# Pairs of up tiles by seven products in the first quarter of the MLP, sums of x behind the activations, and value products by twos

## The chip, the cores and the metric

The kernel runs on one core of a Trainium2 chip. The metric is the device time of one execution in microseconds. The engines are TensorE (PE in the profile; PEld is its loading of weights), VectorE (DVE), ScalarE (ACT), GpSimd (POOL) and SyncE (SP), which only issues transfers. Each engine takes its instructions in the order in which the program has them, and waits for another by semaphores.

## The reference

One inference step of a two-layer encoder with D = 1024 features and 576 tokens (512 of a prompt, 64 of a running stream). Layer 0 mixes tokens by causal pooling over windows, layer 1 by sparse attention: an indexer selects keys, then softmax attention with 16 heads, 4 key heads, runs over them. Each layer is followed by an MLP with squared ReLU. Cut to what matters here:

```python
h = _rmsnorm(x, g)                       # x: 576 x 1024
u = jnp.square(jax.nn.relu(h @ w_up))    # 1024 -> 4096
x = x + u @ w_down                       # 4096 -> 1024
...
s = jnp.where(valid[:, :, None, None, :], s, NEG)
p = jax.nn.softmax(s, axis=-1).astype(v.dtype)
o = jnp.einsum('btgrk,btkgd->btgrd', p, vg)
```

## The kernel before

Features lie on the partitions and tokens in the free dimension: x is eight tiles of 128 x 576, handled in two halves of 288 tokens. Every product of the MLP is made in fp32r from operands that are split into an upper and a lower part, so that a product of a 128 x 128 block of weights with 288 tokens takes three matmuls (upper by upper, upper by lower, lower by upper). ScalarE casts the upper part (L192 for weights, L490 for activations), VectorE or GpSimd subtracts it to get the lower part (L193, L493). In the text a lower is that subtraction.

`mlp` goes over the 4096 hidden features in four quarters of eight up tiles, each followed by its share of the down product. In quarters 1 to 3 two up tiles make a pair, and `seven` gets a pair by seven products of half-size blocks where plain work has eight; the down products of all quarters are made so too. Such a group is 7 products x 4 tiles x 3 matmuls = 84 matmuls; two plain tiles are 96. The products, in the order of their work, are b11, t1, t2, b21, t3, b22, t4. Three PSUM banks (a, b, c) gather them. The operands t1, t2, t4 are sums of x: `x_sums` makes them for a tile j by one scaled copy on ScalarE (L449), four fused VectorE rows of 288 columns (L450 to L453), one cast of 864 columns (L454) and one lower of 864 columns (L455, tile xt). t3 is a difference, kept in `snap` (L451) and split by `x_difference` into the first half of xs[j], which the plain products read until then.

In the first quarter all eight up tiles are plain: `project` (L325) runs 8 x 3 x 2 = 48 matmuls a tile. The first two are done before the normalisation's factor is known: its statistics are asked for behind tile 1, and TensorE spreads the factor over the partitions (rb, L355) inside tile 2; ScalarE copies it to SBUF (rbm, L356). Then `finished` takes each tile: the activation (L477 for a tile in two banks, L479 for one in a pair of banks), which frees the tile's PSUM, the square (L471), the sums of the activations (L501 to L514) and their split. The sums of x follow behind tiles 3 and 5 (j = 0, 1), and inside the first two groups of down products (j = 2, 3, in `x_prepared`).

Weights come as a stream of blocks in the order of `mlp_jobs`. A block of kind "up" is used as it is. A pair of blocks, "even" and "odd", is turned into the seven weight operands of a pair: some of them are sums of blocks, made by accumulating transfers on GpSimd's queue (L234, L255) or by VectorE (L280, L284). `Stream.fill` issues the transfers as there is room.

A scheduler of the framework places the instructions on each engine; `behind` and `issue_after` put an instruction behind given others. The order in the built program therefore differs from that of the code.

In the attention, `values` (L1422, L1429, L1435) multiplies the probabilities with V, for each query block i and each key head group in two steps s = 0, 1. For i = 2, 3 each step writes half of a PSUM tile o with outputs of 64 partitions, two heads apart by 64; for the block of the running stream (i = 4) the last of five key tiles has 64 rows.

## Time and profile before

| what | before |
|---|---|
| time, median of 3 runs (lowest to highest) | 1066.94 us (1066.5 to 1067.46) |
| the profiled execution, in all | 1068.9 us |
| its span | 1065.8 us |
| mean granted TensorE clock | 0.995 |

The profile is of one execution, taken on the core. Its page gives the busy time of each engine, the chain of work that ended last, the costliest groups of instructions (line, engine, operation, output<-inputs, shape, count, then busy us, mean ns of one and idle us ahead of it with what ended it), and the transfers. Behind it the trace can be asked for the rows of any engine in a stretch of time, for the chain in order of time, and for a table of windows.

### The profile page before, as it was taken

Reading aid. Unit: us, or ns where it says so; the run is one execution under the profiler, and the core shown is the slowest. Engines: PE = TensorE matmul, PEld = TensorE weight load, DVE = VectorE, ACT = ScalarE, POOL = GpSimd, SP = SyncE. Lnnn points to the kernel's source line nnn. Section 1 sums busy time; section 2 is a strip of 40 time slices with the busy share of each in tenths; the row PEclk is TensorE's granted clock in tenths of the full one; section 3 lists DMA queues with packets and bytes.
Section 4 is the critical chain, followed back from the end, with each engine's and each line's share of the span. In section 5 each row is a group of like instructions: output and inputs, shape, how many; then the busy total and the mean of one; then the engine's idle time right before and its main releaser. Section 6 shows DMA issues by size and latency. Waiting matters only on the chain.

```text
span 1065.8 us, 21684 instructions
## 1 busy us (share of the span) xinstructions
PE 1045.2 (98%) x7970; PEld 1023.4 (96%) x7970; DVE 910.7 (85%) x1865; ACT 624.7 (59%) x1252; POOL 237.6 (22%) x254
## 2 busy tenths in 40 slices
PE   8999999999999999999999999999999999999996
PEld 8999999999999999999989889999999999999995
DVE  7879989879978998889999675689989979979984
ACT  8546557547646765354368786455467447547742
POOL 3200111111111110667556711000111111111101
PEclk9999999999999999999999999999999999999998
DMA  8334676676576665845542545343665676676522
GB/s 251 91 99 100 167 173 152 168 172 161 146 182 169 156 174 170 238 129 149 169 149 78 180 134 149 119 110 88 181 166 141 178 177 161 150 187 158 127 54 89
DMA packets 98027, 159.64 MB, mean 150 GB/s; under 512 B 15697, under 2 KB 29312, under 8 KB 97920
## 3 DMA queue, kind: packets, MB, share of 16 engines
q1 hardware_dynamic: 70720, 111.78, 33.3%
q0 software_dynamic: 15840, 28.84, 17.1%
q10 hardware_dynamic: 11360, 17.63, 5.2%
q8 instruction: 62, 1.02, 0.4%
q14 instruction: 45, 0.37, 0.1%
HBM read 142.99 MB, written 12.72 MB: 146 GB/s over the span
## 4 chain that ended last, share of the span: by engine, by line
PE 85%; DVE 7%; DMA 3%; issue 2%; POOL 2%; ACT 1%; SPq 0%; ACTq 0%; DVEq 0%; POOLq 0%
PE b L527 31%; PE c L527 16%; PE up L325 9%; PE a L527 8%; PE pj L325 5%; PE wo L325 3%; PE wa L325 2%; PE pb L1067 1%; PE pt L1397 1%; PE o L1429 1%; DMA raw<-in_w_in 1%; PE dn L325 1%; DVE mask L1314 1%; PE sc L1371 1%; DVE wl L193 1%
## 5 line engine op out<-in xcount | busy, mean ns | idle before, releaser
L192 ACT CAST wh<-raw 128x512 fp32r<-128x512 f32 x308 | 189.4, 619 | 196.0 <-PE b L527 63.2
L193 DVE TENSOR_TENSOR wl<-raw,wh 128x512 fp32r<-128x512 f32 x284 | 197.4, 697 | 33.7 <-ACT wh L192 29.4
L527 PE MATMUL b<-u,wh 128*128 128x288 f32 x992 | 202.1, 295 | 0.4 <-DVE u L493 0.4
L527 PEld LDWEIGHTS b<-u,wh 128*128 128x128 f32 x992 | 159.6, 188 | 1.3 <-DVE u L493 0.7
L192 ACT CAST wh<-sum 128x512 fp32r<-128x512 f32 x165 | 102.0, 620 | 95.2 <-PE b L527 33.7
L527 PE MATMUL b<-u,wl 128*128 128x288 f32 x496 | 145.3, 295 | 0.4 <-DVE wl L193 0.4
L193 DVE TENSOR_TENSOR wl<-sum,wh 128x512 fp32r<-128x512 f32 x165 | 112.1, 685 | 18.7 <-ACT wh L192 17.2
L527 PE MATMUL c<-u,wh 128*128 128x288 f32 x496 | 102.6, 296 | 0.0
L255 POOL DMA_DIRECT2D sum<-in_w_down x31 | 27.1, 894 | 327.4 <-DMA sum<-in_w_down 124.9
L527 PEld LDWEIGHTS b<-u,wl 128*128 128x128 f32 x496 | 93.2, 188 | 0.6 <-DVE wl L193 0.6
L325 PE MATMUL up<-xs,wh 128*128 128x288 f32 x512 | 89.3, 295 | 0.2
L493 DVE TENSOR_TENSOR u<-v,u 128x576 fp32r<-128x576 f32 (+3 forms) x106 | 82.7, 786 | 3.5 <-ACT u L490 3.1
L527 PEld LDWEIGHTS c<-u,wh 128*128 128x128 f32 x496 | 79.7, 188 | 1.3 <-ACT wh L192 1.1
L527 PE MATMUL b<-xt,wh 128*128 128x288 f32 x384 | 78.0, 296 | 1.3 <-DVE v L664 1.3
L527 PE MATMUL b<-xs,wh 128*128 128x288 f32 x384 | 77.3, 295 | 0.0
L490 ACT CAST u<-v 128x576 fp32r<-128x576 f32 (+3 forms) x106 | 73.4, 699 | 4.0 <-DVE v L514 3.2
L325 PEld LDWEIGHTS up<-xs,wh 128*128 128x128 f32 x512 | 74.7, 188 | 1.0 <-DVE v L479 0.7
L527 PE MATMUL c<-u,wl 128*128 128x288 f32 x248 | 73.2, 295 | 0.0
L255 POOL DMA_DIRECT2D sum<-in_w_up x24 | 20.8, 865 | 201.7 <-DVE wl L193 77.5
L527 PEld LDWEIGHTS b<-xt,wh 128*128 128x128 f32 x384 | 61.5, 188 | 1.8 <-DVE v L664 1.8
L325 PE MATMUL pj<-xs,wh 128*128 128x288 f32 x352 | 62.1, 295 | 0.0
L527 PEld LDWEIGHTS b<-xs,wh 128*128 128x128 f32 x384 | 61.2, 188 | 0.0
(298 smaller groups left out, 2723.4 us busy)
## 6 DMA issues: line engine op xcount, KB each, us to landing
raw<-in_w_up SPq DMA_DIRECT2D x128, 256.0 KB, 3.0
raw<-in_w_down SPq DMA_DIRECT2D x128, 256.0 KB, 2.8
raw<-in_w_o ACTq DMA_DIRECT2D x32, 256.0 KB, 2.7
sum<-in_w_down SPq DMA_DIRECT2D x31, 256.0 KB, 2.8
sum<-in_w_down POOLq DMA_DIRECT2D x31, 256.0 KB, 4.4
raw<-in_w_down POOLq DMA_DIRECT2D x31, 256.0 KB, 4.9
raw<-in_w_in ACTq DMA_DIRECT2D x30, 256.0 KB, 3.1
sum<-in_w_up SPq DMA_DIRECT2D x24, 256.0 KB, 3.0
```

What stands on the lines that cost most here:

```text
L192: cast(h, src)
L193: (sub or how["sub"]).tensor_tensor(l, src, f32(h), ALU.subtract)
L255: pool.dma_start(s1, odd[:, 512:], accum_op=ALU.add)
L325: pe.matmul(pt[h][:, :m] if isinstance(pt, tuple) else pt[:, h, :m], wt, xs[k][:, part, c:c + m], start=(k == 0 and i == 0), stop=(k == n ...
L490: return act.copy(u[:, f, 0], v[:, f])
L493: return dve.tensor_tensor(u[:, f, 1], v[:, f], f32(u[:, f, 0]), ALU.subtract)
L527: ins = pe.matmul(bank[:, :HT], wt, ut, start=first and j == 0 and i == 0, stop=j == 3 and i == 2, skip_group_check=True)
L1067: pe.matmul(pt[:, c0:c0 + rhs.shape[1]], lhs, rhs, start=n == 0, stop=n == len(steps) - 1)
L1314: dve.match_replace(order[rows], m8[rows], order[rows], TAKEN)
L1371: pe.matmul(pt[:, hh, :nw], q[:, 2 * s + hh], ks[g][:, part, :nw], start=part == 0, stop=part == 1)
L1397: pe.transpose(pp[:, c:c + P], pr[:, hh, kt * P:(kt + 1) * P], ident)
L1429: pe.matmul(o[64 * hh:64 * hh + 64, s * P:(s + 1) * P], V[:, kt, vs], pT[:, c:c + P], start=kt == 0, stop=kt == i)
```

## The change

Of the eight up tiles of each first quarter, the first four stay plain (`PLAIN_UP`); the last four become two pairs by `seven`, so that the stream's blocks of these are "even" and "odd". All sums and differences of x stand before those pairs: `x_sums(0)` behind the statistics' last sum, `x_sums(1)` and `x_sums(2)` behind the activation of tile 1, `x_sums(3)` at tile 3. The lowers of j = 0, 1 go to GpSimd; so does the second lower of three of the four plain blocks. The difference is written to `rough[:, j]`, and `x_prepared` is gone. Apart from the MLP, `values` makes both steps of a group at s = 1 for i = 2, 3, and the last key tile of i = 4 uses all 128 rows, those of the padding set to zero.

```diff
+PLAIN_UP = 4
+POOLED = (1, 2, 3)
...
-                kind = "odd" if c and n % 2 else "even" if c else "up"
+                kind = "up" if not c and n < PLAIN_UP else "odd" if n % 2 else "even"
...
+                if kind == "even" and "sums" not in phase:
+                    return
...
+                pooled = kind == "up" and (ups - 1) % PLAIN_UP in POOLED
...
-                dve.tensor_tensor(self.s2, self.s2, sq, ALU.add)
+                self.added = dve.tensor_tensor(self.s2, self.s2, sq, ALU.add).ins
...
-        def x_sums(j, raw, first, difference):
+        def x_sums(j):
...
+            at = half * (1 + j % 2)
+            raw, first, difference = rough[:, at:at + 3], rough[:, at + 3], rough[:, j]
...
-            dve.tensor_tensor(t[:, :, 1], raw, f32(t[:, :, 0]), ALU.subtract)
+            (pool if j < 2 else dve).tensor_tensor(t[:, :, 1], raw, f32(t[:, :, 0]), ALU.subtract)
...
-                dve.scalar_tensor_tensor(v, pt[:, :, :HT], 0.0, halves(norm.rb), ALU.max, ALU.mult)
+                active[:] = [dve.scalar_tensor_tensor(v, pt[:, :, :HT], 0.0, halves(norm.rb), ALU.max, ALU.mult).ins]
...
-        for i in range(KT):
+        for i in range(PLAIN_UP):
...
             if i == 1:
                 norm.stats()
+                with behind([norm.added]):
+                    x_sums(0)
             if i < 2:
                 continue
+            if i == 3:
+                x_sums(3)
             for t in todo:
                 finished(*t)
             todo.clear()
...
+            if i == 2:
+                snap = halves(tmp("snap", "s2", 1))
+                with behind(active):
+                    x_sums(1)
+                    x_sums(2)
+        for j in range(half):
+            x_difference(j, rough[:, j])
+        for j in range(PLAIN_UP // 2, half):
+            up = Up(0, j)
+            seven(of_x, False, up)
+            us.append(up.u)
...
-        for n, q in enumerate(FIRST_DOWN):
-            seven(of(us), n == 0, Down(q))
-            x_prepared(n)
+        for q in FIRST_DOWN:
+            seven(of(us), q == FIRST_DOWN[0], Down(q))
...
+        pool.memset(V[TS:, 8], 0.0)
...
+                        pool.memset(end[TS:, :4 * TS], 0.0)
...
-                if s == 0:
+                if s == (TURNED <= i < 4):
                     self.group.o = psum1("o")
+                if TURNED <= i < 4 and s == 0:
+                    self.group.pT = pT
+                    return
...
-                    for kt in range(i + 1):
-                        for hh in range(2):
-                            c = (kt * 2 + hh) * P
-                            pe.matmul(o[64 * hh:64 * hh + 64, s * P:(s + 1) * P], V[:, kt, vs], pT[:, c:c + P], start=kt == 0, stop=kt == i)
+                    for j, t in enumerate((self.group.pT, pT)):
+                        for kt in range(i + 1):
+                            for hh in range(2):
+                                c = (kt * 2 + hh) * P
+                                pe.matmul(o[64 * hh:64 * hh + 64, j * P:(j + 1) * P], V[:, kt, vs], t[:, c:c + P], start=kt == 0, stop=kt == i)
```

The lines of the kernel move by a few: the weight lower L193 becomes L195, the sums of x L450 to L455 become L460 to L465, the activations L477 and L479 become L489 and L491, the sums of activations L501 to L514 become L513 to L526, the matmuls L325 and L527 become L333 and L539, the split of xs L312 becomes L320, and the value products L1429 become L1437.

The first place is VectorE, from the first activation in the first quarter of layer 0 on. A number behind a name tells one buffer from another: up_687 and up_748 are tiles 0 and 1, up_832 and up_833 the two halves of tile 2. Before:

```order
L479 SCALAR_TENSOR_TENSOR v_891<-up_687,rbm_149_866 128x2x288
L479 SCALAR_TENSOR_TENSOR v_891<-up_748,rbm_149_866 128x576
L193 TENSOR_TENSOR wl_917<-raw_401,wh_916 128x512
L501 TENSOR_TENSOR v_891<-v_891 128x288
L508 SCALAR_TENSOR_TENSOR v_891<-v_891 128x288
L511 TENSOR_TENSOR v_891<-v_891 128x288
L514 SCALAR_TENSOR_TENSOR v_891<-v_891 128x288
L493 TENSOR_TENSOR u_892<-v_891,u_892 128x3x288
L493 TENSOR_TENSOR u_892<-v_891,u_892 128x4x288
L193 TENSOR_TENSOR wl_992<-raw_407,wh_991 128x512
L477 SCALAR_TENSOR_TENSOR v_905<-up_832,rbm_149_866 128x288
L477 SCALAR_TENSOR_TENSOR v_905<-up_833,rbm_149_866 128x288
```

With the change tiles 0 and 1 are up_677 and up_756, and tile 2 is up_845 and up_846. The order starts with the same activations:

```order
L491 SCALAR_TENSOR_TENSOR v_904<-up_677,rbm_151_879 128x2x288
L491 SCALAR_TENSOR_TENSOR v_904<-up_756,rbm_151_879 128x576
L460 SCALAR_TENSOR_TENSOR rough_676<-x_81,gv,rough_676 128x288
L461 SCALAR_TENSOR_TENSOR rough_676<-x_83,gv,rough_676 128x288
L460 SCALAR_TENSOR_TENSOR rough_676<-x_82,gv,rough_676 128x288
L461 SCALAR_TENSOR_TENSOR rough_676<-x_84,gv,rough_676 128x288
L195 TENSOR_TENSOR wl_945<-raw_731,wh_944 128x512
L513 TENSOR_TENSOR v_904<-v_904 128x288
L462 SCALAR_TENSOR_TENSOR rough_676<-x_83,negative_674,rough_676 128x288
L195 TENSOR_TENSOR wl_1048<-raw_733,wh_1047 128x512
L462 SCALAR_TENSOR_TENSOR rough_676<-x_84,negative_674,rough_676 128x288
L505 TENSOR_TENSOR u_905<-v_904,u_905 128x3x288
```

and comes to the activation of tile 2 (up_845, up_846) 18 rows further on:

```order
L195 TENSOR_TENSOR wl_1107<-raw_738,wh_1106 128x512
L465 TENSOR_TENSOR xt_932<-rough_676,xt_932 128x3x288
L460 SCALAR_TENSOR_TENSOR rough_676<-x_82,gv,rough_676 128x288
L505 TENSOR_TENSOR u_905<-v_904,u_905 128x4x288
L462 SCALAR_TENSOR_TENSOR rough_676<-x_84,negative_674,rough_676 128x288
L489 SCALAR_TENSOR_TENSOR v_918<-up_845,rbm_151_879 128x288
L489 SCALAR_TENSOR_TENSOR v_918<-up_846,rbm_151_879 128x288
L491 SCALAR_TENSOR_TENSOR v_918<-up_954,rbm_151_879 128x576
```

Before, eight rows stand between the activation of tile 1 and that of tile 2; now there are 27, among them the sums of x for j = 1, 2 and part of j = 3, the differences' lowers (L320) and five weight lowers.

The second place is TensorE behind tile 3 of the first quarter of layer 0. Before, the plain tiles follow one another (up_923 is tile 3, up_1006 tile 4):

```order
L325 MATMUL up_923<-xs_660,wh_742 128x288 x4
L325 MATMUL up_923<-xs_660,wl_743 128x288 x2
L325 MATMUL up_923<-xs_663,wh_742 128x288 x4
L325 MATMUL up_923<-xs_663,wl_743 128x288 x2
L325 MATMUL up_1006<-xs_642,wh_817 128x288 x4
L325 MATMUL up_1006<-xs_642,wl_818 128x288 x2
L325 MATMUL up_1006<-xs_645,wh_817 128x288 x4
L325 MATMUL up_1006<-xs_645,wl_818 128x288 x2
```

With the change the pair's products stand there (up_954 is tile 3; b_1031, a_1032, c_1033 are the banks of the first pair, xt_825, xt_924, xt_932 the sums of x for j = 0, 1, 2):

```order
L539 MATMUL a_1032<-xs_650,wh_944 128x288 x2
L539 MATMUL a_1032<-xs_650,wl_945 128x288
L539 MATMUL a_1032<-xs_653,wh_944 128x288 x2
L539 MATMUL a_1032<-xs_653,wl_945 128x288
L539 MATMUL b_1031<-xt_924,wh_940 128x288 x2
L539 MATMUL b_1031<-xt_924,wl_941 128x288
L539 MATMUL b_1031<-xt_932,wh_940 128x288 x2
L539 MATMUL b_1031<-xt_932,wl_941 128x288
L539 MATMUL c_1033<-xt_825,wh_841 128x288 x2
L539 MATMUL c_1033<-xt_825,wl_842 128x288
L539 MATMUL c_1033<-xt_924,wh_841 128x288 x2
L539 MATMUL c_1033<-xt_924,wl_842 128x288
```

The products t2 and t1 read xt_825, xt_924 and xt_932 within 21 matmuls of tile 3's end; before, the first products that read a sum of x stood behind the down products, a whole quarter later. The pair's first product (b_1031 from xs_632 to xs_641) stands ahead of tile 3.

The third place is TensorE in the attention, at a group of value products for i = 2. Before, the two steps of o_7715 stand apart:

```order
L1371 MATMUL sc_7700<-k_6064,q_7618 128x384 x4
L1429 MATMUL o_7715<-pT_7655,V 64x128 x6
L1397 MATMUL pt_7766<-ident,p_7627 128x128 x6
L1371 MATMUL sc_7776<-k_6064,q_7618 128x384 x4
L1429 MATMUL o_7715<-pT_7691,V 64x128 x6
L1397 MATMUL pt_7838<-ident,p_7663 128x128
```

With the change the two steps of a group, o_7820, follow each other:

```order
L333 MATMUL wa_7757<-ot_7687,wl_7065 128x256
L1437 MATMUL o_7820<-pT_7691,V 64x128 x6
L1437 MATMUL o_7820<-pT_7727,V 64x128 x6
L1374 MATMUL sc_7884<-k_6105,q_7724 128x384 x3
L1400 MATMUL pt_7901<-ident,p_7735 128x128 x4
L333 MATMUL wa_7833<-ot_7238,wh_7070 128x256 x2
```

The products of the first step moved behind the transposes of the second. Of the four groups of i = 2 one stood so before, and all four do now; in those of i = 3 other rows still stand between the steps.

More of the change, by code (lines that the diff above doesn't have):

```diff
@@ L262, in made @@
         stream = Stream()
+        ups = 0
         while True:
@@ L270, in made @@
                 turns["out"] += kind == "w_o"
+                if kind == "up":
+                    ups += 1
+                pooled = kind == "up" and (ups - 1) % PLAIN_UP in POOLED
                 for i in range(2):
-                    u = split_unit(raw[i], kind == "w_kq" and i == 0 and turns["spare"] < SPARE_UNITS, pool if early or kind == "w_kq" and i else None,
+                    u = split_unit(raw[i], kind == "w_kq" and i == 0 and turns["spare"] < SPARE_UNITS, pool if early or i and (pooled or kind == "w_kq") else None,
                                    pool.tensor_copy if early and i else act.copy)
@@ L471, in square @@
             act.activation(v, v, AF.Square)
+        active = []
         def activated(pt, v):
@@ L711, in finished @@
             activated(pt, v[:, 5:7] if i % 2 else v[:, 1:5:3])
-            if i == KT - 2:
-                parts_of(u, v, slice(4, 5))
-                first_sum(v)
-                parts_of(u, v, slice(2, 3))
-            elif i == KT - 1:
-                middle_sums(v)
-                parts_of(u, v, slice(1, 4, 2))
-                upper(u, v, slice(5, 7))
-                last_sum(v)
-                lower(u, v, slice(5, 7))
-                parts_of(u, v, slice(0, 1))
-            elif i % 2:
+            if i % 2:
                 upper(u, v, slice(4, 7))
@@ L746, in mlp @@
             todo.clear()
-            if i in (3, 5):
-                r = 2 * i - 6
-                if i == 3:
-                    snap = halves(tmp("snap", "s2", 1))
-                x_sums(i // 2 - 1, rough[:, r:r + 3], rough[:, r + 3], snap[:, i // 2 - 1])
-        def x_prepared(n):
-            if n < 2:
-                v = v_tile()
-                x_difference(n, snap[:, n])
-                x_sums(n + 2, v[:, :3], v[:, 3], v[:, 4])
-                x_difference(n + 2, v[:, 4])
-        for n, q in enumerate(FIRST_DOWN):
-            seven(of(us), n == 0, Down(q))
-            x_prepared(n)
+            if i == 2:
[11 more added lines that the diff above has]
+            seven(of(us), q == FIRST_DOWN[0], Down(q))
         for c in range(1, 4):
@@ L1433, in values @@
                             c = (kt * 2 + hh) * P
-                            lhs, rhs = (V[:, 4 + kt, vs], pT[0][:, c:c + P]) if kt < 4 else (V[:TS, 8, vs], pT[1][:TS, c - KT * P:c - KT * P + P])
+                            lhs, rhs = (V[:, 4 + kt, vs], pT[0][:, c:c + P]) if kt < 4 else (V[:, 8, vs], pT[1][:, c - KT * P:c - KT * P + P])
                             pe.matmul(o[64 * hh:64 * hh + 64, :P], lhs, rhs, start=kt == 0, stop=kt == 4)
```

## The prediction

> **What bounds the kernel now.** I read the page's header, the chain that ended last by engine, and the busy times. The profiled execution took 1068.9 us in all, of which the span is 1065.8, so 3.1 us lie around it; it stands 1.96 us above the median of the runs (1066.94).
>
> ```profile
> span 1065.8 us, 21684 instructions
> PE 1045.2 (98%) x7970; PEld 1023.4 (96%) x7970; DVE 910.7 (85%) x1865; ACT 624.7 (59%) x1252; POOL 237.6 (22%) x254
> PE 85%; DVE 7%; DMA 3%; issue 2%; POOL 2%; ACT 1%; SPq 0%; ACTq 0%; DVEq 0%; POOLq 0%
> ```
>
> TensorE is busy for 98% of the span, so a matmul taken away is worth its time, provided that nothing is late behind it. VectorE at 85% is the engine to watch. The chain of waits in order of time shows the first quarter of the MLP, layer 0 and then layer 1 (start, length, work):
>
> ```profile
> 41.80 12.77 PE up L325 x96
> 55.74 5.36 PE up L325 x39
> 63.35 19.30 PE up L325 x144
> 82.91 12.69 PE up L325 x96
> 139.79 3.17 PE b L527 x24
> 699.57 19.30 PE up L325 x144
> 719.14 12.69 PE up L325 x96
> ```
>
> 96 matmuls take 12.77 us, or 0.133 us each. From 63.35 to 139.79 stand the last five up tiles (240 matmuls) and four groups of seven down products (336); 576 times 0.133 is 76.6 us, and the rows leave 76.4. So TensorE has no wait at all in the first quarter now. The windows (start:end, length, busy time of PE, PEld, DVE, ACT, POOL, then clock, DMA share, GB/s) show who else is full there:
>
> ```profile
> 55.00:69.00 14.00, 13.91 (x100) 13.25 (x100) 9.86 (x21) 6.21 (x12) 1.75 (x2) 1.00 0.34 95
> 69.00:83.00 14.00, 14.00 (x108) 14.00 (x107) 13.76 (x26) 9.18 (x14) 0.70 (x1) 1.00 0.41 112
> 83.00:96.00 13.00, 13.00 (x101) 13.00 (x100) 11.12 (x19) 6.97 (x13) 0.16 (x1) 1.00 0.26 52
> 678.00:691.00 13.00, 13.00 (x101) 13.00 (x100) 4.94 (x8) 4.23 (x7) 0.00 (x0) 1.00 0.33 109
> 705.00:719.00 14.00, 14.00 (x108) 14.00 (x108) 13.77 (x27) 8.96 (x14) 0.09 (x1) 1.00 0.37 103
> ```
>
> VectorE is busy for 13.76 of 14 us just behind the point where the normalisation is known, in both layers alike, and has room ahead of it (4.94 of 13 in layer 1). The change puts more VectorE work, with a nearer due time, exactly into the full stretch.
>
> **What is saved.** Four plain tiles are 4 x 48 = 192 matmuls; two groups of seven products are 2 x 84 = 168. That is 24 fewer a layer, 24 x 0.133 = **-3.2 us**, and -6.4 for two layers. Nothing is saved on VectorE: a pair needs seven weight lowers for four and two sums of weights besides.
>
> **What VectorE must now do before TensorE may go on.** The release of the first activation and the rates of VectorE come from its timeline (start, length, row):
>
> ```profile
> 62.54 1.42 DVE L479 SCALAR_TENSOR_TENSOR v<-up,rbm 128x576 f32<-128x576 f32 x2 [2.26 <-ACT rbm L356]
> 63.88 0.68 DVE L193 TENSOR_TENSOR wl<-raw,wh 128x512 fp32r<-128x512 f32 x1
> 64.47 0.45 DVE L501 TENSOR_TENSOR v<-v 128x288 f32<-128x288 f32 x1
> 69.33 0.81 DVE L477 SCALAR_TENSOR_TENSOR v<-up,rbm 128x288 f32<-128x288 f32 x2
> ...
> 72.99 1.05 DVE L493 TENSOR_TENSOR u<-v,u 128x864 fp32r<-128x864 f32 x1
> 73.96 0.51 DVE L450 SCALAR_TENSOR_TENSOR rough<-x,gv,rough 128x288 f32<-128x288 f32 x1
> 74.39 0.51 DVE L451 SCALAR_TENSOR_TENSOR snap<-x,gv,rough 128x288 f32<-128x288 f32 x1
> 76.71 1.35 DVE L493 TENSOR_TENSOR u<-v,u 128x1152 fp32r<-128x1152 f32 x1
> 77.98 0.51 DVE L452 SCALAR_TENSOR_TENSOR rough<-x,negative,rough 128x288 f32<-128x288 f32 x1
> 698.76 1.42 DVE L479 SCALAR_TENSOR_TENSOR v<-up,rbm 128x576 f32<-128x576 f32 x2 [1.97 <-ACT rbm L356]
> ```
>
> Rows overlap by about 0.08 us, so I count from start to start: an activation of 576 columns 0.67 (62.54 to 63.88, two rows), a weight lower 0.59 (63.88 to 64.47), a fused row of 288 columns 0.43 (73.96 to 74.39), a lower of 864 columns 0.97 (72.99 to 73.96), one of 1152 columns 1.27 (76.71 to 77.98). A plain sum of 288 columns gets 0.37, its 0.45 less the overlap.
>
> In the new order, 29 VectorE rows stand from the first activation up to the row ahead of the activation of tile 2's first half (v from up_845), and that activation makes 30. They are 2 activations of 576 (1.34), 14 fused rows of 288 columns, eleven of them sums of x (6.02), 6 plain sums and lowers of 288 (2.22), 5 weight lowers (2.95), 2 lowers of 864 (1.94) and one of 1152 (1.27): 15.74, or 15.8 us with hardly a wait between them. The new wait behind the activations thus holds the sums back until 62.8, and on an engine that takes its rows in order everything else queues behind them. The normalisation's two matmuls stand two places later than before, 0.27 us, so VectorE starts at 62.8 and that activation is done at **78.6**.
>
> It frees the bank that the product t1 of the first pair writes (c_1033). TensorE's rows ahead of it, from the old 63.35, are tile 3 (48), the pair's first product (12) and 21 matmuls of t2 and b21: 81 x 0.133 = 10.8, so it would be there at **74.1**. The wait is 78.6 - 74.1 = **4.5 us**, more than the 3.2 saved. Before the change both halves of that activation were done at 70.1 (69.33 and 0.81), since no sum of x stood ahead of them.
>
> Behind it, TensorE does c's 9 matmuls, 12 of the next pair and 2 with the upper half of the fourth sum, 23 x 0.133 = 3.1, and stands at 81.7 before the matmul that needs the lower half. VectorE has four fused rows, one activation of 576, two plain sums, a small row and the lower of 864 to do until then, 1.72 + 0.67 + 0.74 + 0.1 + 0.97 = 4.2, so 82.8. **1.1 us** more. ScalarE's part of that chain is the next price:
>
> ```profile
> 79.77 0.91 ACT L454 CAST xt<-rough 128x864 fp32r<-128x864 f32 x1
> 89.56 1.15 ACT L490 CAST u<-v 128x1152 fp32r<-128x1152 f32 x1
> ```
>
> Two casts of 864 (0.9 each), one of 1152 (1.15), two weight casts and a copy stand one behind the other before the copy that the pair's next product waits for: I work it to 84.7 where TensorE is at 83.35, **1.3 us**, and the same kind of wait at the second pair's end and at the first down product, 1.0 and 0.3. These 2.6 are the least certain terms; they lie between nothing and 4. Together 4.5 + 1.1 + 2.6 = 8.2 a layer.
>
> **The lowers on GpSimd.** Two lowers of 864 columns a layer and three weight lowers go to GpSimd. The trace has such rows, and what VectorE did beside them:
>
> ```profile
> 455.74 1.42 POOL L1171 TENSOR_TENSOR rp<-rp,sn 128x576 f32<-128x576 f32 x1
> 455.79 1.92 DVE L193 TENSOR_TENSOR wl<-raw,wh 128x512 fp32r<-128x512 f32 x1
> ...
> L193 DVE TENSOR_TENSOR wl<-raw,wh 128x512 fp32r<-128x512 f32 x284 | 197.4, 697 | 33.7 <-ACT wh L192 29.4
> L193 POOL TENSOR_TENSOR wl<-raw,wh 128x512 fp32r<-128x512 f32 x32 | 41.3, 1310 | 21.6 <-ACT wh L192 21.6
> ```
>
> GpSimd took 1.42 for 576 columns, so 2.1 for 864. VectorE's weight lower, 0.697 as a rule, took 1.92 where it started just behind a GpSimd row: it stood still for 1.2 of that row's 1.42. So moving a lower is not free for VectorE. The three weight lowers stand ahead of the normalisation, where VectorE has room, and I cost them at nothing; without that cover each would be 1.31 instead of 0.70 on the way of a weight. Of the two lowers of 864 the first (xt[0]) runs while VectorE waits for the normalisation. The second (xt[1]) comes behind its cast, which I put at 73.2 by ScalarE's rows in the new order, and ends at about 75.4, among VectorE rows with both inputs in SBUF: they slip by up to its length. Bounds: nothing (GpSimd waits for a gap instead) and 2.1; I take **2.0**, since the nearest pair of rows shows the block. With it the stall is 10.2 a layer. The Trainium skill's page SBUF — State Buffer, section Who interferes with whom, says that a VectorE instruction with two SBUF inputs contends with a GpSimd instruction that reads SBUF, and that the second to issue blocks until the first is done. The rows at 455.7 agree (1.92 against 0.697); by that rule the term is the 2.0 taken, without it 0.
>
> **Value products.** The rows of these groups stand thus in the chain (the trace has two for each matmul of the program), and a GpSimd memset in the groups:
>
> ```profile
> 573.60 0.81 PE o L1429 x12
> 585.64 1.46 PE o L1429 x24
> ...
> L881 POOL MEMSET late<- 128x224 f32 x2 | 0.6, 287 | 0.0
> ```
>
> 24 in a row cost 1.46 where 12 cost 0.81: twice 0.81 less 1.46 is 0.16, the price of a group of its own. Of the four pairs of i = 2 three stood apart and now stand together: -3 x 0.16 = **-0.5 us**; the pairs of i = 3 still stand apart in the new order. Bounds 0 and -1.8 (eleven such gaps). I cost the memsets for the full 128 rows at nothing: they stand on GpSimd, 237.6 of 1065.8 us busy, ahead of the products; without that cover each would be some 0.29 us, as the row of 224 columns.
>
> **Sum.** A layer -3.2 + 8.2 + 2.0 = +7.0; two layers +14.0; less 0.5: +13.5. Layer 1 has the same order, its first activation at 698.76 and its tile 3 at 699.57, as in layer 0, so it counts the same. 1068.9 + 13.5 = 1082.4 for a profiled execution, **1080.4** on the median.
>
> **Rivals.**
> - *No block by GpSimd.* For it: GpSimd's row may fall into one of VectorE's waits. Then +5.0 a layer, +9.5: 1076.4.
> - *Only the bank wait counts.* What comes behind the first stall is absorbed, since VectorE and ScalarE run on while TensorE waits. 2 x (4.5 - 3.2) - 0.5 = +2.1: 1069.0. Against it: VectorE's rows are the very thing that TensorE waits for, so it gains no lead meanwhile.
> - *The faster side.* The pairs come without a wait: 2 x -3.2 - 0.5 = -6.9, so 1060.0. The one place that decides is the activation of tile 2's first half: it must be done at 74.1, not 78.6. That needs the 30 rows in 11.3 us, 0.38 a row where they take 0.53. For it: VectorE is idle for 1.9 us between 83 and 96, and 8 us of layer 1's window ahead, so the sums have where to go. Against: in the new order eleven rows of the sums and five weight lowers do stand in between.
> - *Late weights.* The pairs' blocks need accumulating transfers on GpSimd's queue, which land later than SyncE's. A weight lower at the head of VectorE's rows would wait for one:
>
> ```profile
> sum<-in_w_down SPq DMA_DIRECT2D x31, 256.0 KB, 2.8
> ...
> raw<-in_w_down POOLq DMA_DIRECT2D x31, 256.0 KB, 4.9
> ```
>
> By the difference, 2.1 a layer, it would be 1084.6. Against it: a DMA share of 0.26 to 0.41 in these windows leaves room, and the kernel holds these blocks' transfers back only until the phase of the sums.
> - *The change doesn't do what it says.* The order shows 24 fewer matmuls a layer, so this can only hit the value products, and is inside their bounds.
>
> **How the numbers follow.** Forecast as summed 0.56; no block 0.17; only the bank wait 0.10; late weights 0.10; the faster side 0.07. Together the low ends of the unknown costs (2.6 at nothing and 2.0 at nothing in both layers, and -1.8) give 1069.9, the bank wait alone 1069.0; the high ends (4 for 2.6, and the late weights) 1080.4 + 2.8 + 4.2 = 1087.4. So the range is 1069 to 1087, which leaves out the faster side. About 0.2%, 2.1 us, is what a measurement of this kernel can tell from no change; the bank-wait case lies on that edge, so I give it half to same and half to slower, and of the others nothing to same but 0.02: faster 0.07, same 0.07, slower 0.86.
>
> **What would show it.** Right: TensorE idle of 4 to 7 us between about 73 and 79 (and 709 to 715), before the t2 and t1 products that read xt, put down to the sums' lowers or to the activation of tile 2; VectorE busy without a gap from 62.8 to 83; quarter 1 starting about 7 us later; 48 matmuls fewer in all. The block: a GpSimd lower of 864 columns of about 2.1 us with a VectorE row of over 2 us beside it. Wrong: VectorE's rows shorter than in the old rows, the activation of tile 2 done by 75, or TensorE reaching t1 later than 74 for another reason, which would take from the stall what it adds ahead of it.

## The result, and the profile after

The changed kernel takes 1079.1 us (median of 4 runs, 1077.45 to 1080.63), the kernel before 1067.2 beside it: a ratio of 1.0115, 95% interval 1.0102 to 1.0128. The forecast was 1080.4. The profiled execution took 1079.16 us with a span of 1077.4. Its page:

```profile
span 1077.4 us, 21726 instructions
PE 1046.8 (97%) x7922; PEld 1022.5 (95%) x7922; DVE 928.2 (86%) x1895; ACT 636.9 (59%) x1288; POOL 267.3 (25%) x275
```

TensorE has 48 matmuls fewer (7922 for 7970), VectorE 17.5 us more work. Where the time went is read from four landmarks in TensorE's timeline: the first up matmul of the first MLP, the first statistics of layer 1, the first up matmul of the second MLP, the first statistics of the final normalisation. Before:

```profile
41.64 0.77 PE L325 MATMUL up<-xs,wh 128*128 128x288 f32 x4
422.13 1.34 PE L375 MATMUL st<-ones,s 128*128 128x96 f32 x10
677.94 0.68 PE L325 MATMUL up<-xs,wh 128*128 128x288 f32 x4
1043.82 0.67 PE L375 MATMUL st<-ones,s 128*96 128x96 f32 x6
```

With the change:

```profile
41.81 0.77 PE L333 MATMUL up<-xs,wh 128*128 128x288 f32 x4
429.92 1.34 PE L383 MATMUL st<-ones,s 128*128 128x96 f32 x10
685.45 0.69 PE L333 MATMUL up<-xs,wh 128*128 128x288 f32 x4
1058.05 0.67 PE L383 MATMUL st<-ones,s 128*96 128x96 f32 x6
```

The first MLP went from 380.49 to 388.11 (+7.62), the attention between them from 255.81 to 255.53 (-0.28), the second MLP from 365.88 to 372.60 (+6.72), and the end of the program, from the last landmark to the end of the span, from 21.98 to 19.35 (-2.63). With 0.17 at the start that is 11.6, the difference of the spans. So the loss is in the two MLPs, 14.3 us, and 2.6 of it come back at an end that the change doesn't touch. The -0.28 of the attention is the sum of two differences of opposite sign (see the value products).

Inside the first quarter TensorE waits where it never waited before. The windows (columns as before):

```profile
69.00:83.00 14.00, 8.37 (x48) 7.79 (x48) 12.08 (x26) 6.18 (x9) 6.67 (x3) 0.77 0.46 109
...
719.00:733.00 14.00, 9.69 (x50) 9.11 (x51) 12.00 (x20) 7.33 (x14) 4.28 (x3) 0.76 0.36 76
```

Both layers lose the same way: TensorE is busy for 8.37 and 9.69 of 14 us, and its granted clock is at 0.77 and 0.76. In layer 0 its timeline has four waits (in brackets: idle before the row, and who ended it):

```profile
78.06 0.61 PE L539 MATMUL b<-xt,wh 128*128 128x288 f32 x1 [4.58 <-POOL xt L465]
...
80.68 0.85 PE L539 MATMUL c<-xt,wh 128*128 128x288 f32 x2 [1.05 <-DVE v L489]
...
81.56 0.69 PE L539 MATMUL c<-xt,wh 128*128 128x288 f32 x2
82.04 0.45 PE L539 MATMUL c<-xt,wl 128*128 128x288 f32 x1
...
87.81 0.53 PE L539 MATMUL c<-xs,wh 128*128 128x288 f32 x2 [0.55 <-ACT snap L661]
...
102.76 0.54 PE L539 MATMUL b<-xt,wh 128*128 128x288 f32 x2 [0.73 <-ACT v L675]
```

Together 6.9 us. Besides, the 30 matmuls from 78.06 to 86.8 stand 0.24 us apart instead of 0.133 (81.56 to 82.04 are two), 3.2 us more. 6.9 + 3.2 - 3.2 saved is 6.9, of the 7.6 that the first MLP lost; the other 0.7 isn't followed.

VectorE's timeline at that place:

```profile
62.97 1.42 DVE L491 SCALAR_TENSOR_TENSOR v<-up,rbm 128x576 f32<-128x576 f32 x2 [1.79 <-ACT rbm L364]
...
73.16 0.45 DVE L526 SCALAR_TENSOR_TENSOR v<-v 128x288 f32<-128x288 f32 x1
73.53 0.68 DVE L195 TENSOR_TENSOR wl<-raw,wh 128x512 fp32r<-128x512 f32 x1
...
75.10 1.05 DVE L465 TENSOR_TENSOR xt<-rough,xt 128x864 fp32r<-128x864 f32 x1
78.04 0.52 DVE L460 SCALAR_TENSOR_TENSOR rough<-x,gv,rough 128x288 f32<-128x288 f32 x1 [1.90 <-POOL xt L465]
...
80.18 0.81 DVE L489 SCALAR_TENSOR_TENSOR v<-up,rbm 128x288 f32<-128x288 f32 x2
```

and GpSimd's work in layer 0, with VectorE's rows beside the first of its two lowers of sums and beside a weight lower ahead of it:

```profile
51.16 1.61 DVE L461 SCALAR_TENSOR_TENSOR rough<-x,gv,rough 128x288 f32<-128x288 f32 x1
...
54.78 2.02 POOL L465 TENSOR_TENSOR xt<-rough,xt 128x864 fp32r<-128x864 f32 x1 [2.33 <-ACT xt L464]
55.25 2.10 DVE L195 TENSOR_TENSOR wl<-sum,wh 128x512 fp32r<-128x512 f32 x1 [0.90 <-ACT wh L194]
...
73.03 4.97 POOL L465 TENSOR_TENSOR xt<-rough,xt 128x864 fp32r<-128x864 f32 x1 [15.41 <-ACT xt L464]
```

The first lower of a sum takes GpSimd 2.02 us, and it is VectorE that stands still: its weight lower, started 0.47 us later, takes 2.10 instead of 0.68. At 51.16 too a VectorE row takes 1.61 instead of 0.51, beside a weight lower of GpSimd of 1.29 from 51.17. Both stand ahead of the normalisation, where no wait of TensorE follows. The second lower of a sum, started at 73.03 while VectorE ran row behind row, takes 4.97: there the five VectorE rows that start behind it keep their usual length (0.45, 0.68, 1.05), and GpSimd is done 1.85 us after VectorE's row of 75.10 has ended, which is about its own length over again. So here it was GpSimd that stood still, until VectorE itself had to wait (1.90 us) for the buffer that GpSimd was reading. Layer 1 has the same 4.97. The Trainium skill's page SBUF — State Buffer, section Who interferes with whom, has one of two such instructions block the other for its whole length, by who issued first. The rows at 54.78 and 55.25 agree; those from 73.03 on don't, as VectorE's rows that start later by the trace run ahead of GpSimd's. VectorE's next row stood ready at 51.16 as well, so what decides who gets in isn't shown.

### The profile page after: what moved, and what is told of

It reads as the page before. It is cut to its first block, busy times and chain, and to the rows that moved or that the text cites. A ratio compares the mean times of both kernels' runs of the same rounds, so it can differ in the third digit from the quotient of the medians.

```text
span 1077.4 us, 21726 instructions
## 1 busy us (share of the span) xinstructions
PE 1046.8 (97%) x7922; PEld 1022.5 (95%) x7922; DVE 928.2 (86%) x1895; ACT 636.9 (59%) x1288; POOL 267.3 (25%) x275
## 4 chain that ended last, share of the span: by engine, by line
PE 81%; DVE 9%; issue 2%; ACT 2%; DMA 2%; POOL 2%; SPq 0%; ACTq 0%; DVEq 0%; POOLq 0%
PE b L539 34%; PE c L539 17%; PE a L539 8%; PE pj L333 5%; PE up L333 4%; PE wo L333 3%; PE wa L333 2%; DVE mask L1317 1%; PE pb L1069 1%; DVE m L1316 1%; DVE p L1341 1%; PE dn L333 1%; DVE wl L195 1%; POOL xt L465 1%; PE o L1437 1%
## 5 line engine op out<-in xcount | busy, mean ns | idle before, releaser
L195 DVE TENSOR_TENSOR wl<-raw,wh 128x512 fp32r<-128x512 f32 x280 | 195.6, 699 | 23.4 <-ACT wh L194 19.1
L539 PE MATMUL b<-u,wh 128*128 128x288 f32 x992 | 203.1, 296 | 0.4 <-DVE u L505 0.4
L539 PEld LDWEIGHTS b<-u,wh 128*128 128x128 f32 x992 | 160.0, 188 | 1.6 <-DVE u L505 0.6
L539 PE MATMUL b<-u,wl 128*128 128x288 f32 x496 | 146.0, 296 | 0.4 <-DVE wl L195 0.4
L195 DVE TENSOR_TENSOR wl<-sum,wh 128x512 fp32r<-128x512 f32 x177 | 121.6, 693 | 28.7 <-ACT wh L194 27.2
L539 PE MATMUL b<-xt,wh 128*128 128x288 f32 x448 | 93.0, 299 | 10.5 <-POOL xt L465 9.2
L539 PE MATMUL c<-u,wh 128*128 128x288 f32 x496 | 103.0, 297 | 0.0
L539 PEld LDWEIGHTS b<-u,wl 128*128 128x128 f32 x496 | 93.5, 189 | 0.6 <-DVE wl L195 0.6
L539 PE MATMUL b<-xs,wh 128*128 128x288 f32 x448 | 92.2, 300 | 0.0
L505 DVE TENSOR_TENSOR u<-v,u 128x576 fp32r<-128x576 f32 (+2 forms) x108 | 83.0, 773 | 2.5 <-ACT u L502 2.1
L539 PEld LDWEIGHTS b<-xt,wh 128*128 128x128 f32 x448 | 72.9, 191 | 11.4 <-POOL xt L465 9.6
L539 PEld LDWEIGHTS c<-u,wh 128*128 128x128 f32 x496 | 79.7, 188 | 1.8 <-ACT wh L194 1.5
L502 ACT CAST u<-v 128x576 fp32r<-128x576 f32 (+2 forms) x108 | 73.8, 689 | 4.0 <-DVE v L526 2.1
L539 PEld LDWEIGHTS b<-xs,wh 128*128 128x128 f32 x448 | 73.3, 192 | 0.0
L539 PE MATMUL c<-u,wl 128*128 128x288 f32 x248 | 73.2, 295 | 0.0
L539 PE MATMUL b<-xt,wl 128*128 128x288 f32 x224 | 66.7, 298 | 0.0
L539 PE MATMUL b<-xs,wl 128*128 128x288 f32 x224 | 65.1, 299 | 0.0
L481 ACT ACTIVATE v<-v 128x288 f32<-128x288 f32 (+1 forms) x120 | 53.5, 458 | 18.2 <-DVE v L489 10.7
```

The source lines that it names most:

```text
L195: (sub or how["sub"]).tensor_tensor(l, src, f32(h), ALU.subtract)
L481: act.activation(v, v, AF.Square)
L502: return act.copy(u[:, f, 0], v[:, f])
L505: return dve.tensor_tensor(u[:, f, 1], v[:, f], f32(u[:, f, 0]), ALU.subtract)
L539: ins = pe.matmul(bank[:, :HT], wt, ut, start=first and j == 0 and i == 0, stop=j == 3 and i == 2, skip_group_check=True)
```

## The experiments

In the tables, MLP 0 and MLP 1 are the stretches between the landmarks in each run's profiled execution, and end is from the last landmark to the end of the span.

### The lowers back on VectorE

```diff
-            (pool if j < 2 else dve).tensor_tensor(t[:, :, 1], raw, f32(t[:, :, 0]), ALU.subtract)
+            dve.tensor_tensor(t[:, :, 1], raw, f32(t[:, :, 0]), ALU.subtract)
```

> The lowers of the sums of x for j = 0, 1 on VectorE instead of GpSimd, all else as in the changed kernel. Theory G (GpSimd is starved: its lower of xt[1] took 4.97 us beside a VectorE that never stopped, against 2.02 for the first one, and both TensorE and VectorE then wait for it): the wait before the second part of t2 falls from 4.58 to about 2.5 us, VectorE's 1.90 us of idle at 78 goes, the activation of tile 2 is done at about 79.3 instead of 80.6; the two first waits together 4.3 instead of 5.6 a layer, so 1076 us. Theory V (VectorE's row of work alone sets the wait, GpSimd's help is worth its length): two more lowers of 0.97 on VectorE a layer, the activation of tile 2 later than 80.6 by 1 us or more, 1081 to 1083 us.

1075.96 us, ratio 1.0087 (1.0072 to 1.0102); MLP 0 386.64, MLP 1 371.77, which is 1.5 and 0.8 less than with the change. TensorE's timeline in the first quarter:

```profile
75.54 0.40 PE L539 MATMUL b<-xt,wh 128*128 128x288 f32 x1 [2.12 <-DVE xt L465]
77.11 0.54 PE L539 MATMUL b<-xt,wh 128*128 128x288 f32 x1 [0.91 <-DVE xt L465]
79.18 0.85 PE L539 MATMUL c<-xt,wh 128*128 128x288 f32 x2 [1.28 <-DVE v L489]
```

4.31 us in place of 5.63, as theory G had it: the help of GpSimd cost more than it gave. But three quarters of the loss are left (0.87% of 1.15%), and these three waits all name VectorE; the two behind them, 0.61 and 0.99 us, name ScalarE as before.

### The sums earlier, and more cover ahead of the pairs

Two ways to give the sums of x more time: behind the statistics instead of the activation,

```diff
                 with behind([norm.added]):
                     x_sums(0)
+                    x_sums(1)
+                    x_sums(2)
...
-                with behind(active):
-                    x_sums(1)
-                    x_sums(2)
```

> x_sums(1) and x_sums(2) stand with x_sums(0) behind the statistics' last sum, not behind the activation of tile 1; all else as in the changed kernel. Theory Q (what costs is the place of the sums in VectorE's row, between the activation of tile 1 and that of tile 2): VectorE has 19 rows there instead of 29, some 10.5 us, so the activation of tile 2 is done at about 74.5, where TensorE needs it at 74 to 75: waits under 1 us a layer, no slow matmuls, 1061 to 1065 us, faster than the kernel before. Rival N (VectorE is full wherever the sums stand): the sums delay the normalisation's factor, which stands 8 matmuls later on TensorE, and the first activation with it; waits of 2 to 4 us a layer stay, 1070 to 1075 us.

and six plain tiles with one pair:

```diff
-PLAIN_UP = 4
+PLAIN_UP = 6
```

> Six plain tiles and one pair by seven products in each first quarter, instead of four and two. The saving is half, 12 matmuls or 1.6 us a layer, and TensorE has 96 matmuls (12.8 us) more ahead of the first product that reads a sum of x. Theory Q (the due time is the cost): no wait over 0.5 us, no slow matmuls, 1067.2 - 3.2 - 0.3 = 1063.7 us. Rival P (the pair's own chain, weights and the copies between its products, is the cost): waits of 2 us or more a layer around the pair stay, 1068 to 1072 us.

Both failed: 1078.12 us, 1.0108 (1.0093 to 1.0123), and 1078.5 us, 1.0108 (1.0093 to 1.0123), slower than theory Q and than either rival had it. The waits only moved. With the sums early:

```profile
65.89 0.85 PE L539 MATMUL b<-xs,wh 128*128 128x288 f32 x2 [2.20 <-ACT rbm L364]
89.03 0.55 PE L539 MATMUL b<-xt,wh 128*128 128x288 f32 x2 [3.88 <-DVE v L676]
```

With six plain tiles:

```profile
77.87 0.51 PE L539 MATMUL c<-xt,wh 128*128 128x288 f32 x2 [0.43 <-DVE v L489]
...
96.03 0.40 PE L539 MATMUL b<-u,wh 128*128 128x288 f32 x1 [1.75 <-DVE u L505]
99.46 0.85 PE L539 MATMUL b<-xt,wh 128*128 128x288 f32 x2 [2.90 <-ACT v L675]
```

The wait for the activation of tile 2 is gone in one and down to 0.43 in the other; in its place TensorE waits for the normalisation, or at the last pair and the first down product. So theory Q, that one place in VectorE's row is the price, falls. What the three arrangements have in common is that all of VectorE's work for the pairs is due before their last products. In the changed kernel the window from the first activation to the second pair's last product (62.97 to 102.76) has VectorE busy for 36.77 of 39.79 us; before, a window of the same length has it busy just as long, but TensorE has 300 matmuls there in place of 217:

```profile
62.97:102.76 39.79, 32.88 (x217) 31.82 (x216) 36.77 (x69) 25.13 (x46) 8.42 (x5) 0.87 0.38 91
...
62.54:102.30 39.76, 39.67 (x300) 39.44 (x299) 36.73 (x64) 24.90 (x40) 3.36 (x4) 1.00 0.35 92
```

So a full VectorE alone is not the price; what is new is how much of its work TensorE's next products need. Theory S: that sum of work is what TensorE waits for, wherever its rows stand.

### TensorE kept busy through the wait

34 matmuls that nobody reads, into a free bank, behind b21 and ahead of the second part of t2; the rows of VectorE stay as they are.

```diff
+                    with behind([ins.ins]):
+                        for n in range(FILLER):
+                            pe.matmul(spare[:, 0, :HT], t2[0][:, :P], xs[0][:, 0, HT:], start=n == 0, stop=n == FILLER - 1, skip_group_check=True)
```

> The changed kernel with 34 matmuls more a layer (4.5 us, a product nobody reads, into a free bank) where TensorE stands idle, behind the first part of b21 and ahead of the second part of t2. VectorE's and GpSimd's rows are the same. Theory C (the granted clock falls because TensorE stood idle, and the 30 matmuls behind the wait pay 0.24 instead of 0.133 us): they take 0.133, and the time falls by up to 3.2 us a layer, to 1073 to 1075 us, although TensorE does 68 matmuls more. Rival D (the slow matmuls have another cause, such as their operands): they stay at 0.24, and the time is 1079 to 1080 us.

1080.1 us, 1.0131 (1.0114 to 1.0148): the time is about rival D's. The window and the timeline:

```profile
69.00:83.00 14.00, 12.18 (x90) 11.71 (x89) 12.04 (x26) 6.67 (x10) 6.73 (x3) 1.00 0.45 106
...
80.20 0.53 PE L540 MATMUL c<-xt,wh 128*128 128x288 f32 x2 [1.68 <-DVE v L490]
84.29 0.40 PE L540 MATMUL c<-xt,wh 128*128 128x288 f32 x1 [0.79 <-DVE xt L466]
85.95 0.53 PE L540 MATMUL c<-xs,wh 128*128 128x288 f32 x2 [0.86 <-ACT snap L674]
90.14 0.54 PE L540 MATMUL b<-xt,wh 128*128 128x288 f32 x2 [0.73 <-ACT a L573]
101.61 0.54 PE L540 MATMUL b<-xt,wh 128*128 128x288 f32 x2 [0.47 <-ACT v L688]
```

Theory C is right on the clock: it stays at 1.00, and the matmuls behind the wait take their usual time. But nothing is gained: TensorE comes sooner to operands that aren't there, and waits 0.79, 0.86, 0.73 and 0.47 us where the slow matmuls had filled the time. The low clock was covered by VectorE's work, which agrees with S.

### Work taken away from VectorE

The changed kernel without the sums of x for j = 1, 2, 3:

```diff
         def x_sums(j):
+            if j:
+                x_sums_tile()
+                xt.append(xt[0])
+                return
```

> The changed kernel with the sums of x for j = 1, 2, 3 left out: all four j read the sum of j = 0, in every quarter, so the products t1, t2, t3, t4 are of wrong operands; TensorE's work is the same. Theory S (VectorE's whole work between the first activation and the first down product is what TensorE waits for, wherever its rows stand; the sums of x are the part that the change moved into that stretch): VectorE is relieved of 3 x 4 x 0.43 + 2 x 0.97 = 7.1 us a layer, the waits of 6.9 us a layer and the slow matmuls behind them go but for about 1 us, and the time is 1060 to 1063 us, below the kernel before. Rival W (the pairs' seven weight lowers and sums of weights, or the copies between their products, are the price): waits of 3 us or more a layer stay, 1068 to 1073 us.

and the kernel before with the same left out:

> The control: the kernel before with the same sums of x (j = 1, 2, 3) left out, all j reading that of j = 0. TensorE had no wait in its first quarters, so by either theory nothing is gained: 1065 to 1068 us, less than 0.2% from the kernel before. A gain of several us here would mean that the sums cost TensorE something before the change as well, and that the run without them in the changed kernel tells nothing of the change.

| run | time, us | ratio (interval) | MLP 0 | MLP 1 | end |
|---|---|---|---|---|---|
| without three sums, changed | 1061.81 | 0.9953 (0.9936 to 0.9969) | 378.88 | 365.82 | 19.28 |
| without three sums, before | 1065.53 | 0.9986 (0.9977 to 0.9995) | 379.84 | 365.35 | 22.09 |

The change without the sums is 17.3 us faster than with them (16.0 of it in the two MLPs), the kernel before 1.1 us. One wait a layer is left (1.88 and 1.89 us); in layer 0:

```profile
82.46 0.53 PE L543 MATMUL b<-xt,wh 128*128 128x288 f32 x2 [1.88 <-DVE v L680]
```

So the sums of x, due before the pairs, are most of what the change pays with; the weight lowers and the copies between products alone leave 1.9 us. The run takes away the sums' copies and casts on ScalarE and GpSimd's second lower too, so it doesn't show VectorE's share by itself. The gain of one against the other is less than the 3.2 us a layer of the saving: 1.0 in layer 0, none in layer 1 (365.82 against 365.35). In layer 1 the 17 matmuls behind the wait stand 0.22 us apart instead of 0.133, about 1.5 us more; the granted clock was 0.93 and 0.95 in the two windows of 14 us there.

### Sums where VectorE is idle

If S holds, the sums cost nothing where VectorE would stand idle: 8 us ahead of the normalisation in layer 1. The next run puts them at the start of each MLP, with six plain tiles and all lowers of sums on VectorE (the calls at the former places are gone):

```diff
         todo, us = [], []
+        for j in range(3):
+            x_sums(j)
         for i in range(PLAIN_UP):
...
```

> An arrangement by theory S: six plain tiles and one pair; the sums of x for j = 0, 1, 2 stand at the start of the MLP, free to fill VectorE's idle time there (about 6 us in layer 0, over 8 us in layer 1); all lowers of sums on VectorE. By S the waits of 5.4 us a layer of the run with six plain tiles shrink by the idle time used, nearly all in layer 1 and half in layer 0, and the time is 1064 to 1069 us. If instead the sums at the start delay the normalisation (rival N), the first activation comes 1 to 3 us later, and the time stays at 1072 to 1078 us.

1068.77 us, 1.0020 (1.0010 to 1.0029). Layer 1's MLP takes 364.77, 1.1 less than before the change; layer 0's 385.55, 5.1 more. The waits are all at the normalisation, one in each layer:

```profile
58.11 2.02 PE L383 MATMUL st<-ones,s 128*128 128x96 f32 x8 [4.11 <-DVE s L351]
...
704.97 0.81 PE L333 MATMUL up<-xs,wh 128*128 128x288 f32 x4 [0.75 <-DVE v L491]
```

Theory and rival N each hold in one layer; how much of the gain over the run with six plain tiles is due to the lowers on VectorE, this run doesn't tell. So two runs change layer 1 alone, with one pair and with two; layer 0 is that of before.

> The kernel before, with one pair by seven products (six plain tiles) in the first quarter of layer 1 alone, its sums for j = 0, 1, 2 at the start of that MLP, all lowers on VectorE; layer 0 as before. In the run with the sums first in both layers, layer 1's MLP took 364.8 us against 365.9 before, and layer 0's 385.6 against 380.5. Theory S: layer 1 has the idle VectorE time for the sums and layer 0 hasn't, so 1.1 us are gained and nothing lost: 1064.5 to 1066 us, or 1062 to 1063.5 if the end of the program is also 2.6 us shorter, as in all runs so far with the changed MLP. If VectorE's work in layer 1 had been relieved by something that layer 0 did differently in that run, the MLP of layer 1 takes 366 us or more.

> The same with two pairs (four plain tiles) in the first quarter of layer 1 alone. Twice the saving, 3.2 us, and more VectorE work due earlier. By theory S VectorE's deficit in that stretch, some 5 us a layer in the changed kernel, is relieved by three sums, 3 x 1.72 + 2 x 0.97 = 7.1 us, as far as they find idle time (8 us before the normalisation): layer 1's MLP in 362.7 to 365 us, time 1063 to 1066 us. Rival (the pair's own chain): waits of 2 us or more at the pairs, MLP of layer 1 at 366 us or more.

| run | time, us | ratio (interval) | MLP 0 | MLP 1 | end |
|---|---|---|---|---|---|
| one pair in layer 1 | 1066.11 | 0.9991 (0.9982 to 1.0000) | 380.50 | 365.39 | 22.17 |
| two pairs in layer 1 | 1066.22 | 0.9992 (0.9983 to 1.0000) | 380.49 | 368.20 | 19.49 |

One pair gains 0.5 us in the MLP where theory S had 1.1, two lose 2.3 where it had gains. A wait stands again at the first pair's last product, until VectorE has taken the one before it out of the bank:

```profile
720.79 0.54 PE L534 MATMUL b<-xt,wh 128*128 128x288 f32 x2 [3.88 <-DVE v L671]
```

This is the rival's case: a wait of over 2 us at the pairs and an MLP of over 366 us. Of the sums and differences of x only lowers stand behind the first activation there (one of 1.05 us, four of 0.45); VectorE's other rows, weight lowers, sums of weights and of activations and their lowers, fill the rest. So with the sums made ahead the pairs still wait for VectorE: theory S misses in this, that idle time for the sums is enough. Neither run beats the kernel before by what can be told (0.2%).

### The value products

The kernel before with the new value products, and the changed kernel with the old ones:

> The kernel before with the change of the value products alone (and the memsets for it). Expected from the prediction: three of four groups of i = 2 come together, 0.5 us, bounds 0 and 1.8; from the traces, where the attention of the changed kernel was 0.28 us shorter from the first to the second MLP: 0.3 us. Both are below what the time can tell: 1065 to 1068 us; the trace's stretch between the end of the first MLP and the start of the second tells them apart.

> The changed kernel with the value products of before. By the traces (the attention 0.28 us shorter with the change) the time is that of the changed kernel plus 0.3 us, ratio 1.0115 to 1.013. If the value products by twos cost 2.2 us, as the times of the run with them alone say, it is 1.009 to 1.010.

1068.87 us, 1.0021 (1.0011 to 1.0032), and 1076.93 us, 1.0092 (1.0078 to 1.0106) where the whole change has 1.0115 (1.0102 to 1.0128): by twos the products cost some 2 us, which the first run shows and the second, whose interval overlaps, agrees with. The whole stretch from the first MLP to the second says the opposite, 255.56 us with them alone against 255.81 before. But it holds a wait ahead of these groups,

```profile
451.02 0.40 PE L1266 MATMUL wi<-ident,wib 32*64 32x32 f32 x4 [1.52 <-POOL wib L1248]
```

which is 0.19 to 2.44 us in the traces with the old products and missing in that of the run with the new ones alone; why, is open. So the groups themselves have to be compared. In the trace of the run with them alone TensorE's waits at the groups of i = 2 and behind are

```profile
567.05 0.33 PE L1398 MATMUL pt<-ident,p 128*128 128x128 f32 x1 [0.65 <-POOL p L1351]
572.32 0.33 PE L1398 MATMUL pt<-ident,p 128*128 128x128 f32 x1 [0.17 <-POOL p L1351]
572.88 0.77 PE L1398 MATMUL pt<-ident,p 128*128 128x128 f32 x5 [0.23 <-POOL p L1351]
574.72 0.33 PE L1398 MATMUL pt<-ident,p 128*128 128x128 f32 x1 [0.30 <-POOL p L1351]
608.71 0.79 PE L1382 MATMUL sc<-ck,q 128*128 128x288 f32 x4 [0.22 <-ACT pT L1399]
621.61 1.09 PE L1441 MATMUL o<-pT,V 128*64 128x128 f32 x16 [0.38 <-ACT pT L1410]
643.95 1.09 PE L1441 MATMUL o<-pT,V 128*64 128x128 f32 x16 [0.55 <-ACT pT L1410]
```

Before, only the first and the last of these seven are there. From the first to the last it is 76.90 us (567.05 to 643.95), where before it is 75.01:

```profile
568.74 0.33 PE L1397 MATMUL pt<-ident,p 128*128 128x128 f32 x1 [0.67 <-POOL p L1350]
...
643.75 1.09 PE L1435 MATMUL o<-pT,V 128*64 128x128 f32 x16 [0.55 <-ACT pT L1408]
```

With the whole change it is 76.60, with the old products in it 75.20. Of the 1.89 us the three new waits for GpSimd are 0.70, the two new ones for ScalarE 0.60; the rest is in no wait. Two things can have made them, and no run parts them. The first step's products, now put off to the second, had filled TensorE's time while GpSimd scaled the next probabilities. And the new memsets stand in GpSimd's row right ahead of that scaling:

```profile
570.77 0.81 POOL L1406 MEMSET end<- 64x256 f32 x3
571.68 1.15 POOL L1351 TENSOR_SCALAR p<-p,over 128x384 f32<-128x384 f32 x2
```

### The end of the program

> The kernel before, unchanged, as a second look at its end: from the first statistics of the final normalisation to the end of the span it had 22.0 us, where all kernels with the changed MLP have 19.3 to 19.6. If that is the program's own, it is 22 again; if it was that one execution, 19 to 20. The ratio of its times to the kernel before is 1 within 0.2%.

22.06 us from the last landmark to the end, and 0.9999 (0.9990 to 1.0008). So the longer end is the program's own, as far as two executions tell. It doesn't go with the changed MLP either, as the table above shows (22.17 and 19.49 with one pair and two). By the DMA slices of the two traces the last output has landed about 4.6 us before the end before the change and 2.0 with it, and one fetch of instructions stands behind it in both; what decides on the 2.6 us is open.

## Why the prediction was right, point by point

- **What bounds the kernel, and the saving.** As forecast: 48 matmuls fewer, TensorE waiting, VectorE busy through the stretch but for the 1.90 us at 78 (the forecast had no gap).
- **The 30 rows to the activation of tile 2.** Forecast 15.74 us of work from 62.8; they ran from 62.97 to about 80.6 (80.18 and half of 0.81), 17.6 us, of which 1.90 were idle: 15.7.
- **The wait at the first pair.** That 4.58 was measured where 4.5 was forecast is chance. The forecast 4.5 was for the activation of tile 2, which frees the bank of t1; the measured 4.58 stands at t2 and ended with GpSimd's lower, and the wait for the activation was 1.05 behind it. Together the two were to be 4.5 + 2.0 = 6.5 and were 5.6.
- **The lowers on GpSimd.** Mis-told for the lower that counts, with the right size. The step had GpSimd block VectorE for 2.0 at xt[1]; there VectorE kept GpSimd out for 3 us, and then waited for it, 1.90. The block as forecast, 2.02 beside 2.10, is at xt[0], which the step took to run while VectorE waits. Lowering on VectorE gave back 3.1 us (1079.1 to 1075.96).
- **The waits behind (1.1 and 2.6).** Only 0.55 and 0.73 are seen. In their place stand 30 matmuls at a low clock, 3.2 us, which the prediction didn't have. With the clock held up the waits of the forecast are there: 0.79 for the fourth sum, and 0.86 + 0.73 + 0.47 = 2.1 for the 2.6. VectorE's and ScalarE's chain sets the end either way.
- **The sum of a layer.** Forecast +7.0, measured +7.62 and +6.72, out of other terms: 6.9 of waits for 10.2, and 3.2 of slow matmuls for none. That the one makes up for the other is not luck alone, as the run with TensorE kept busy shows: the same chain sets the end.
- **The value products.** Wrong in sign by the times: -0.5 forecast, +2.2 in the run with them alone, and +1.4 to +1.9 in the traces of the groups. The step took each group's own price of 0.16 for the whole effect and didn't ask for whom the products were cover; and it put the memsets at nothing, as standing ahead of the products on an idle GpSimd, where they stand ahead of the scaling that TensorE waits for. Which of the two counts for how much is open.
- **What was not in the sum.** The end of the program, -2.6. It hides about what the value products cost and the MLPs lost beyond the forecast; that the total came so near (1079.1 for 1080.4) is in this part luck.
- **The rivals.** Without a block by GpSimd (1076.4) is in number what the run with the lowers on VectorE came to, 1075.96. That only the bank wait counts (1069.0) is refuted by the time; with the clock held up the waits behind the first are seen. Late weights aren't seen: none of TensorE's waits at the pairs names a weight lower. The faster side needed VectorE's rows in 11.3 us; with three sums left out it is reached, 1061.81, though 2.7 of the 5.1 us below the kernel before are at the end of the program.

## What to carry to other kernels

Where TensorE and a vector engine are both nearly full, count what the vector engine has to finish before each point at which TensorE needs it, not the work as a whole. Here 6.4 us of matmuls were saved and 20.7 paid (14.3 net in the two MLPs), most of it for operands that had been made at leisure before. Moving the same rows about mostly moved the wait, and where the sums found idle time the two pairs' other work still made TensorE wait. Before work is put off in order to be grouped, look for whom it was cover. A helper engine next to one that never pauses may be no help at all: here taking its two lowers back gained 3.1 us.

## What the runs showed of the hardware

- GpSimd's subtraction of 864 columns took 2.02 us where a VectorE row of two SBUF operands started behind it and took 2.10 instead of 0.68. It took 4.97 (4.98 and 5.03 in two other runs) beside a VectorE with a full queue of such rows, five of which ran past it at their usual length.
- TensorE's granted clock fell to 0.77 in the 14 us with waits of 4.58 and 1.05 us, where matmuls of 288 columns stood 0.24 us apart instead of 0.133 for some 9 us, and to 0.69 in an 11 us window of the run with six plain tiles (waits of 1.75 and 2.90). The length of the wait alone doesn't tell: in the run without three sums it stayed at 1.00 in layer 0 with a wait of 1.88, and was 0.93 in layer 1 with one of 1.89. With matmuls that nobody reads in the place of the longest wait it stayed at 1.00.
- From the last landmark on, four programs took 22.0 to 22.2 us to their ends and nine others 19.1 to 19.6, though before the change and with it the last transfer is issued 15.5 us behind that landmark; the one profiled twice had 21.98 and 22.06.
